# RoPE and scores: the last slot of three loads of k is brought in by two small transfers of its own

## The chip, the cores and the metric
The kernel runs on one core of a Trainium2 chip. The metric is the device time of one execution in microseconds (us): the median of 6 runs of the kernel before is 800.83 us (800.23 to 801.45). One further execution was recorded by the hardware profiler. It took 801.19 us, of which 799.4 us lie between its first and its last instruction; that stretch is called the span.

## The reference, cut to what matters
Inputs are q and k of shape [16, 512, 16, 64] (batch, position, head, dimension) in float32 and two tables cos and sin of [512, 32].

```python
def rot(x):                                   # rotary embedding
    x1, x2 = x[..., :32], x[..., 32:]
    return concatenate([x1 * cos - x2 * sin, x1 * sin + x2 * cos], axis=-1)
scores = einsum('bshd,bthd->bsht', rot(q), rot(k))      # [16, 512, 16, 512] float32
```

The output has 268 MB, q and k together have 67 MB: for every byte read, four are written.

## The kernel before, in words
**Tiling.** A batch's 512 positions are laid out as 128 partitions times C = 4 slots, so that position 4p + c stands in partition p and slot c. One load (`load`, L79) brings a whole batch of q or of k, 128 rows of 16 KB in DRAM, into a tile of 128 partitions by 4 slots by 1024 numbers. A slot is thus 4 KB of each row. The output is made in 64 stages, one for each batch and slot; a stage makes 128 x 16 x 512 scores (4 MB) in a tile `st` of the pool `stage`, which has three buffers.

**A stage** (the main loop runs i from 4 to 63) runs over 8 pairs of heads. For each pair TensorE makes two products into PSUM (L166, weights are qT, moving data kT of the batch) and ScalarE copies the pair's scores into `st` (L173). In between, VectorE rotates one slot of q two stages ahead and one slot of k five stages ahead (L106, L107, L111), TensorE transposes a slot of q one stage ahead and a slot of k four stages ahead (L127), and VectorE and ScalarE copy these out of PSUM (L142). At the end of a stage the whole 4 MB are stored by one transfer (L147).

**Order.** Everything is in the order of the program (`manual_schedule`); each engine takes its instructions in that order. All loads and all stores of the main loop are issued by SyncE on one queue (called SPq in the profile), in this order for each batch: three stores, a load of q, a store, a load of k. The load of q for batch b is issued after the third stage of batch b - 2, the load of k for batch b after the last stage of batch b - 3. The pool `in` holds two tiles each of q and of k. A transfer over 128 rows is shared out over 16 DMA engines, 8 rows for each; every DMA engine takes its shares one after another in the order of issue, and each of them adds one to the transfer's semaphore when its share is done. There are eight such semaphores, used in turn.

**Where the waits are.** A store waits for ScalarE's last copy of its stage. A stage's first copy into `st` waits until the store that used this buffer, three stages back, has landed in full, that is, on all 16 engines. A load waits for VectorE and TensorE to have done with the tile that it replaces.

**The last store** is cut in three (L151 to L153): the first 14 heads over all 128 rows, and the last two heads first for 116 rows and then for 12. The three lines that the change repeats in a load have this form already:

```python
nc.sync.dma_start(o[:, :h], st[:, :h])          # L151
nc.sync.dma_start(o[:116, h:], st[:116, h:])    # L152
nc.sync.dma_start(o[116:, h:], st[116:, h:])    # L153
```

Of the kernel before, what the change touches and what calls it, by code (L numbers as in the profile page):

```python
# [10 lines left out]
def kernel(  # L11
# [8 lines left out]
    nc = tc.nc  # L20
# [4 lines left out]
    B, S, H, D = q.shape  # L25
    HD = D // 2
    P = 128
    C = S // P
    HP = H // 2
    NST = B * C  # L30
    G = H // C

    const_pool = ctx.enter_context(tc.tile_pool(name="const", bufs=1))
# [9 lines left out]
    dram = {  # L43
        "q": q.rearrange("b (p c) h d -> b p c h d", c=C),
        "k": k.rearrange("b (p c) h d -> b p c h d", c=C),
    }
# [15 lines left out]
    def load_units(which, head, heads):  # L62
        n = C * heads * D
        t = early[:, used[0] : used[0] + n].rearrange("p (c e) -> p c e", c=C)
        used[0] += n
        src = dram[which][0, :, :, head : head + heads, :]
        nc.sync.dma_start(t.rearrange("p c (h d) -> p c h d", d=D), src)
        for h in range(0, heads, G):
            units[which, (head + h) // G] = t[:, :, D * h : D * (h + G)]

    batches = {}

    def load(which, b):

        if b >= B:
            return
        t = in_pool.tile([P, C, H * D], fp32, tag=which + "_in", name=which + "_sb")
        batches[which, b] = t
        nc.sync.dma_start(t.rearrange("p c (h d) -> p c h d", h=H), dram[which][b])  # L79

    def rope(which, n):


        part = part_pool.tile([P, H * D], fp32, tag="part", name="part")
        if n < C:
            x = units[which, n]
            sv, k1, k2 = "p c (g j) -> p c g j", {"j": HD}, {"j": D}
            cs = cos_t.unsqueeze(2).to_broadcast((P, C, 2 * G, HD))
            ss = ss_v.unsqueeze(2).to_broadcast((P, C, G, D))
            pv = part.rearrange("p (c g j) -> p c g j", c=C, j=D)  # L90
            x5 = x.rearrange("p c (h x j) -> p c h x j", x=2, j=HD)
            p5 = part.rearrange("p (c h x j) -> p c h x j", c=C, x=2, j=HD)
            adds = [(x5[:, :, :, y], p5[:, :, :, 1 - y]) for y in range(2)]
        else:
            x = batches[which, n // C][:, n % C]
            sv, k1, k2 = "p (g j) -> p g j", {"j": HD}, {"j": D}
            cs = cos_t[:, n % C].unsqueeze(1).to_broadcast((P, 2 * H, HD))
            ss = ss_v[:, n % C].unsqueeze(1).to_broadcast((P, H, D))
            pv = part.rearrange(sv, **k2)
            x4 = x.rearrange("p (h x j) -> p h x j", x=2, j=HD)  # L100
            swapped = bass.AP(part.tensor, part.offset + HD, [part.ap[0], (D, H), (-HD, 2), (1, HD)])
            adds = [(x4, swapped)]
        xs, xc = x.rearrange(sv, **k2), x.rearrange(sv, **k1)

        def products():
            nc.vector.tensor_tensor(pv, xs, ss, op=mult)  # L106
            nc.vector.tensor_tensor(xc, xc, cs, op=mult)  # L107

        def sums():
            for y, z in adds:  # L110
                nc.vector.tensor_tensor(y, y, z, op=add)  # L111

        return [products, sums]
# [30 lines left out]
    def store(i, st):  # L144
        o = o_v[i // C, i % C]
        if i < NST - 1:
            nc.sync.dma_start(o, st)  # L147
# [7 lines left out]
    def scores(i, p, st):  # L155
# [18 lines left out]
        if b == 0 and p % 2 == 1:  # L174
            c = p // 2
            nc.sync.dma_start(o_v[0, c, :, G * i : G * (i + 1)], st[:, G * c : G * (c + 1)])
        elif b > 0 and p == HP - 1:
# [10 lines left out]
    with tc.manual_schedule():  # L188
        for t, src in ((cos_t, cos), (sin_t, sin)):
            nc.scalar.dma_start(t, src.rearrange("(p c) j -> p c j", c=C))  # L190
        for head, heads in ((0, G), (G, H - G)):
            load_units("k", head, heads)
            load_units("q", head, heads)
        load("k", 1)
        load("q", 1)
        make_identity(nc, ident)
        nc.scalar.copy(out=ss_t[:, :, 0, :], in_=sin_t)
# [6 lines left out]
        for i in range(C):  # L204
            st = st_first[i] if i < 2 else stage_pool.tile([P, H, S], fp32, tag="stage", name="st")
            if i < C - 1:
                dve = rope("k", i + 1) + rope("q", i + 1) + rope("k", C + i)
                nxt = [("k", i + 1), ("q", i + 1)]
            else:
                dve = rope("q", C) + rope("k", C + i) + rope("q", C + 1) + rope("k", 2 * C)  # L210
                nxt = [("q", C), ("k", C + i)]
            for p in range(HP):
                scores(i, p, st)
                if p in (0, 1) and i > 0:
                    run(dve[:1])
                    dve = dve[1:]
                    transposed("k", C + i - 1, p, nc.vector.tensor_copy)
                if p == 3 and i < 2:
                    load("kq"[i], 2)
                if p in (2, 6):  # L220
                    m = len(dve) - (4 if p == 2 else 2) - (2 if i == C - 1 else 0)
                    run(dve[:m])
                    dve = dve[m:]
                    tr_act(*nxt.pop(0))
            run(dve)
        load("k", 3)


        for i in range(C, NST):
            tr = {}  # L230
            if i + 1 < NST:
                tr[1], tr[3] = ("q", i + 1, 0), ("q", i + 1, 1)
            if i + C < NST:
                tr[5], tr[6] = ("k", i + C, 0), ("k", i + C, 1)
            dve = []
            if i + 2 < NST:
                dve += rope("q", i + 2)
            if i + 1 + C < NST:
                dve += rope("k", i + 1 + C)
# [46 lines left out]
```

## Time and profile before

| what | value |
|---|---|
| median of 6 runs | 800.83 us (800.23 to 801.45) |
| the profiled execution | 801.19 us, span 799.4 us |
| TensorE | busy 691.8 us (87%) |
| VectorE | busy 544.6 us (68%) |
| ScalarE | busy 561.9 us (70%) |
| 16 DMA engines, mean rate over the span | 421 GB/s |
| HBM | 67.24 MB read, 268.44 MB written |
| stores of 4 MB | 59, median 24.0 us from issue to landing |
| loads of k, of 2 MB | 15, median 28.4 us from issue to landing |
| loads of q, of 2 MB | 15, median 27.8 us from issue to landing |

Busy time is that of all instructions of an engine; a DMA share of 1.00 means that all 16 engines had packets under way all the time. The time from issue to landing includes the time for which a transfer stands in line behind those issued before it. Beside the busy times the trace has two records that are used below: each DMA packet with its start, duration and size (without the number of its engine), and each of the 16 additions to a transfer's semaphore with its time.

### The profile page before, as it was taken

The numbers are of one execution on the slowest core, as the hardware profiler recorded it, in microseconds if no ns is written. First come the engines' busy times: TensorE is split into PE (matmuls) and PEld (weight loads), VectorE is DVE, ScalarE is ACT, GpSimd is POOL, SyncE is SP. The second block draws the span as 40 slices with busy tenths as digits, with TensorE's granted clock in tenths as the row PEclk, the third lists the DMA queues.
The fourth block names the chain that finished last, engine by engine and source line by source line (L and its number), as shares of the span: only waits on it lengthen the run. The fifth ranks groups of instructions, "written<-read, shape, count | busy, mean of one in ns | idle before, by whom it ended". The sixth has DMA issues, their size and how long they took to land.

```text
span 799.4 us, 7715 instructions
## 1 busy us (share of the span) xinstructions
PE 691.8 (87%) x3072; PEld 300.3 (38%) x3072; DVE 544.6 (68%) x516; ACT 561.9 (70%) x647; POOL 0.7 (0%) x6
## 2 busy tenths in 40 slices
PE   3989999888979989797897978979789797899970
PEld 2444443333434334343343433434334343343430
DVE  6999988666766768585685856848668486685300
ACT  2978886775858668585785857758567685677870
POOL 0000000000000000000000000000000000000000
PEclk9999999998998999898998989989899898998995
DMA  9999999999999999999999999999999999998996
GB/s 348 391 427 429 436 422 430 426 429 439 423 437 423 428 436 424 437 425 432 433 423 440 430 432 427 434 429 432 432 428 433 424 409 440 422 443 355 419 430 264
DMA packets 17844, 336.17 MB, mean 421 GB/s; under 512 B 1808, under 2 KB 3088, under 8 KB 4240
## 3 DMA queue, kind: packets, MB, share of 16 engines
q1 hardware_dynamic: 17520, 335.55, 98.5%
q8 instruction: 24, 0.39, 0.2%
q10 hardware_dynamic: 288, 0.13, 0.1%
q14 instruction: 12, 0.10, 0.0%
HBM read 67.24 MB, written 268.44 MB: 420 GB/s over the span
## 4 chain that ended last, share of the span: by engine, by line
DMA 49%; PE 37%; DVE 5%; ACT 4%; issue 1%; ACTq 0%
DMA out_dram<-st 49%; PE ps L166 28%; PE bank L127 9%; ACT st L173 4%; DVE part L106 2%; DVE early L111 1%; DMA sin_t<-in_sin_dram 1%; DVE k_sb L111 1%; DVE k_sb L107 1%; DVE early L107 1%; DVE kT_t L142 0%; DVE q_sb L107 0%; DVE q_sb L111 0%; ACTq L281 0%; DVE qT_t L142 0%
## 5 line engine op out<-in xcount | busy, mean ns | idle before, releaser
L173 ACT COPY st<-ps 128x1024 f32<-128x1024 f32 x512 | 495.3, 1018 | 202.5 <-DMA out_dram<-st 109.0
L166 PE MATMUL ps<-kT_t,qT_t 64*128 64x512 f32 x2048 | 549.0, 654 | 69.8 <-ACT st L173 69.8
L166 PEld LDWEIGHTS ps<-kT_t,qT_t 64*128 64x128 f32 x2048 | 185.8, 198 | 258.7 <-issue 139.0
L142 DVE COPY qT_t<-bank 128x512 f32<-128x512 f32 x118 | 81.6, 691 | 202.4 <-PE bank L127 202.4
L127 PEld LDWEIGHTS bank<-ident,q_sb 128*128 128x128 f32 x480 | 55.8, 152 | 103.8 <-issue 101.2
L127 PE MATMUL bank<-ident,q_sb 128*128 128x128 f32 x480 | 87.3, 309 | 0.9 <-PE ps L166 0.9
L127 PEld LDWEIGHTS bank<-ident,k_sb 128*128 128x128 f32 x480 | 50.5, 141 | 95.2 <-DVE k_sb L107 37.1
L127 PE MATMUL bank<-ident,k_sb 128*128 128x128 f32 x480 | 78.7, 287 | 1.6 <-DVE qT_t L142 1.2
L142 ACT COPY kT_t<-bank 128x512 f32<-128x512 f32 x122 | 72.5, 598 | 6.2 <-PE bank L127 6.2
L107 DVE TENSOR_TENSOR q_sb<-q_sb,cos_t 128x1024 f32<-128x1024 f32 x60 | 73.5, 1226 | 2.1
L107 DVE TENSOR_TENSOR k_sb<-k_sb,cos_t 128x1024 f32<-128x1024 f32 x60 | 73.5, 1225 | 2.0
L111 DVE TENSOR_TENSOR k_sb<-k_sb,part 128x1024 f32<-128x1024 f32 x60 | 73.5, 1225 | 2.1
L106 DVE TENSOR_TENSOR part<-q_sb,ss_t 128x1024 f32<-128x1024 f32 x60 | 73.5, 1225 | 2.0
L106 DVE TENSOR_TENSOR part<-k_sb,ss_t 128x1024 f32<-128x1024 f32 x60 | 73.0, 1216 | 0.1
L111 DVE TENSOR_TENSOR q_sb<-q_sb,part 128x1024 f32<-128x1024 f32 x60 | 72.9, 1216 | 0.0
L127 PE MATMUL bank<-ident,early 128*128 128x128 f32 x64 | 10.5, 316 | 13.5 <-DVE early L111 11.6
L127 PEld LDWEIGHTS bank<-ident,early 128*128 128x128 f32 x64 | 8.3, 161 | 18.7 <-issue 15.4
L106 DVE TENSOR_TENSOR part<-early,ss_t 128x1024 f32<-128x1024 f32 x8 | 9.8, 1222 | 6.9 <-ACT ss_t L198 6.8
L111 DVE TENSOR_TENSOR early<-early,part 128x512 f32<-128x512 f32 x16 | 10.3, 687 | 0.2
L107 DVE TENSOR_TENSOR early<-early,cos_t 128x1024 f32<-128x1024 f32 x8 | 9.8, 1225 | 0.3
L142 ACT COPY qT_t<-bank 128x512 f32<-128x512 f32 x10 | 5.7, 617 | 3.2 <-PE bank L127 3.2
L142 DVE COPY kT_t<-bank 128x512 f32<-128x512 f32 x6 | 4.1, 685 | 1.1 <-PE bank L127 1.1
(9 smaller groups left out, 2.8 us busy)
## 6 DMA issues: line engine op xcount, KB each, us to landing
out_dram<-st SPq DMA_DIRECT2D x59, 4096.0 KB, 24.0
k_sb<-in_k_dram SPq DMA_DIRECT2D x15, 2048.0 KB, 28.4
q_sb<-in_q_dram SPq DMA_DIRECT2D x15, 2048.0 KB, 27.8
out_dram<-st SPq DMA_DIRECT2D x16, 1024.0 KB, 13.7
out_dram<-st SPq DMA_DIRECT2D x1, 3584.0 KB, 20.4
early<-in_k_dram SPq DMA_DIRECT2D x1, 1536.0 KB, 9.8
early<-in_q_dram SPq DMA_DIRECT2D x1, 1536.0 KB, 13.0
early<-in_k_dram SPq DMA_DIRECT2D x1, 512.0 KB
```

The lines of the kernel that those rows point to most:

```text
L106: nc.vector.tensor_tensor(pv, xs, ss, op=mult)
L107: nc.vector.tensor_tensor(xc, xc, cs, op=mult)
L111: nc.vector.tensor_tensor(y, y, z, op=add)
L127: nc.tensor.transpose(bank[:, x, :], src, ident)
L142: copy(out=dst, in_=src)
L166: nc.tensor.matmul(out=po, lhsT=lhs[64 * r : 64 * r + 64, :], rhs=rh, start=True, stop=True)
L173: nc.scalar.copy(out=so, in_=si)
```

## The change
In the loads of k for batches 9, 12 and 15, slots 0 to 2 are loaded by one transfer over 128 rows of 12 KB. Slot 3 follows in two transfers: rows 0 to 115, and rows 116 to 127, each row 4 KB. The other 12 loads of k that go through `load`, and all loads of q, are as before. The bytes moved, the tile and all work of the other engines stay as they are; SyncE issues six transfers more, and the use of the eight semaphores shifts along with them.

```diff
+    UNEVEN = (9, 12, 15)
 ...
         t = in_pool.tile([P, C, H * D], fp32, tag=which + "_in", name=which + "_sb")
         batches[which, b] = t
-        nc.sync.dma_start(t.rearrange("p c (h d) -> p c h d", h=H), dram[which][b])
+        d = t.rearrange("p c (h d) -> p c h d", h=H)
+        src = dram[which][b]
+        if which == "k" and b in UNEVEN:
+
+            nc.sync.dma_start(d[:, : C - 1], src[:, : C - 1])
+            nc.sync.dma_start(d[:116, C - 1], src[:116, C - 1])
+            nc.sync.dma_start(d[116:, C - 1], src[116:, C - 1])
+        else:
+            nc.sync.dma_start(d, src)
```

## The prediction
> **What bounds the kernel now.** I read the DMA part of the page first, then the waits, then the busy time in chosen stretches, and last the trace's records of single packets and of the additions to each transfer's semaphore.
>
> The DMA part of the page and the list of waits:
>
> ```profile
> DMA  9999999999999999999999999999999999998996
> ...
> q1 hardware_dynamic: 17520, 335.55, 98.5%
> q8 instruction: 24, 0.39, 0.2%
> ```
>
> ```profile
> PEld ps L166 <- ACT st L173: 115.8, 113, 5.2
> ACT st L173 <- DMA out_dram<-st: 109.0, 35, 5.6
> ```
>
> The DMA engines are full in nearly every slice. ScalarE waits for stores to free a buffer of `st`, and TensorE waits for ScalarE. So transfers set the pace. Which of them, the stretches show (columns: start:end, length, then busy us and instruction counts of PE, PEld, DVE, ACT, POOL, then granted clock, DMA share and GB/s):
>
> ```profile
> 600.00:632.00 32.00, 29.14 (x126) 12.64 (x128) 23.76 (x22) 22.67 (x28) 0.00 (x0) 0.89 1.00 430
> ...
> 728.00:730.00 2.00, 2.00 (x12) 0.97 (x12) 1.93 (x3) 1.86 (x3) 0.00 (x0) 1.00 0.31 131
> 730.00:732.80 2.80, 2.80 (x15) 1.10 (x13) 1.07 (x1) 2.65 (x5) 0.00 (x0) 1.00 0.19 82
> 732.80:740.00 7.20, 7.20 (x38) 3.31 (x38) 4.87 (x5) 6.02 (x8) 0.00 (x0) 1.00 1.02 430
> ...
> 792.00:796.00 4.00, 0.00 (x0) 0.00 (x0) 0.00 (x0) 0.00 (x0) 0.00 (x0) 0.50 0.31 122
> 796.00:799.40 3.40, 0.00 (x0) 0.00 (x0) 0.00 (x0) 0.00 (x0) 0.00 (x0) 0.50 0.04 16
> ```
>
> To 632 us all 16 engines work without a gap. At 728 to 732.8 us most stand idle, and yet some go on; and at the end the last 4 us belong to very few. The engines have drifted apart. The semaphore additions say how far. The store issued at 616.9 us lands first at 633.6 us, and on the 16 engines with these lags behind the first: 0, 0, 0.1, 0.2, 0.5, 1.6, 2.5, 2.8, 2.9, 2.9, 2.9, 3.7, 5.1, 5.2, 6.3 and 12.0 us. One engine is alone at the back. Following packets end to start, its 32 KB store packets take 1.243 us on the mean of the stretch from 74 to 632 us where the others take 1.213; its loads are no slower. Its landings follow each other at 9.9 us a store without a gap, while the fastest, at 9.7, run dry when the next store is issued late:
>
> ```profile
> 695.86 72.44 SPq L147 DMA_DIRECT2D out_dram<-st  x8
> 777.83 0.33 SPq L151 DMA_DIRECT2D out_dram<-st  x1
> 778.75 0.68 SPq L152 DMA_DIRECT2D out_dram<-st  x1
> 779.48 1.17 SPq L153 DMA_DIRECT2D out_dram<-st  x1
> ```
>
> The chain is: the slow engine's share of a store lands, a buffer is free, a stage is made, the next store is issued. At the end the slow engine lands last, at 798.4 us; the engines that hold the 116 rows of L152 land theirs at 796.0 to 796.7 and their last row at 796.9; the rest are done by 792.7.
>
> **What the Trainium skill says.** "DMA: Bandwidth & Descriptors", "Why a DMA increments its semaphore by 16 and not by 1": a transfer from SyncE runs on the largest number of engines up to 16 that divides its row count, the lowest-numbered ones, so 116 rows run on 4 (29 rows each) and 12 rows on 12. The trace agrees: L152 has four additions that come with data, L153 twelve. Same page, "Latency and other measured facts": engines 7 and 15 are usually slower. The trace does show one slow engine. L153's twelve additions include one at 798.4 us and L152's four do not, so it is one of engines 4 to 11. "Runtime: NRT & Kernel Launch", "Instruction fetch mechanics": instructions come in 16 KB blocks by DMA; the trace has 24 such packets, and each holds up one DMA engine by about 1.3 us (0.94 us before the next packet and about 0.4 in it). These are part of the lags above.
>
> **The change part by part.**
>
> *Relief of engines 4 to 11.* A 16 KB load row is recorded at 0.611 us and follows the last by 0.607: 8 rows are 4.86 us. After: 8 rows of 12 KB, estimated at 0.75 x 0.607 = 0.455 us, are 3.64, one 4 KB row is 0.155 (recorded 0.159 in L152), together 3.80. The slow engine gains 1.06 us a load, 3.2 us in three. Engines 12 to 15 gain 1.2 a load.
>
> *Charge on engines 0 to 3.* 3.64 + 29 x 0.155 + 0.155 = 8.29 us for 4.86: 3.43 us more a load, 10.3 us in three. From below nothing speaks for less: L152's packets never took under 0.159. From above: L152's four shares took 5.3 to 6.0 us where 29 x 0.155 is 4.5, stalled at their start while other engines finished; if each of the three loads stalls alike, 3 x 1 us more. I take 10.3 and keep 13.3.
>
> *Issues.* Two more on SyncE per load, 0.7 to 1.2 us each as in L152 and L153. The next instruction there is a store that is issued some 9.6 us after the load (357.75 after 348.16), and waits for ScalarE; behind it nothing is delayed. If that cover were gone it would be 2 us a load. The eight semaphores in turn: each transfer waits for the one eight before it, which was issued about 50 us earlier and lands within some 30; nothing.
>
> *Use of the tile.* Slot 3 of the load issued at 348 us is rotated more than 50 us later and lands at about 382: nothing.
>
> *What is late next: the first four engines.* Their own work from 633.6 us on, for an engine with lag L there: 13 stores of 9.70 (8 x 1.213), 3 loads of 4.87, the 28 KB rows 8.5 (8 x 1.062): 149.2, so 782.8 + L. (Before, the first landing of these rows is at 790.6: the difference was idle, 1.4 us at 634, 5.4 at 728, the rest small.) With the charge 793.1 + L, with L152's and L153's rows 5.5 (the shortest now): 798.6 + L. This work is without gaps and can't be done sooner. Before, the end was 798.4. So the end moves by 0.2 + L, L being the largest lag among engines 0 to 3. The slow engine would be done at 798.4 - 3.2 = 795.2, which then sets nothing.
>
> *L.* The packet records carry no engine number. Four drawn from the 15 have a largest lag up to 1.6 in 15 of 1365 draws, up to 3.7 in 36%, up to 5.2 in 73%, 6.3 in 27%. The 16 KB fetches hit eight engines in turn, three rounds, and the slow one is not among them; if these are engines 0 to 7 in order, the first four have lags 5.2, 2.9, 6.3 and 3.7. I take L = 5.5: the sum is +5.7 us on a span of 799.4 and on 801.19 us of the profiled execution, which is 0.36 above the median of the runs. 800.83 + 5.7 gives 806.5.
>
> **The rivals.**
> 1. *The first four are the front group* (lags to 0.5, five engines): the fetches would have to spare them. Then the end moves by 0.2 to 0.7: 801 to 801.6. For it: on the last stores, where lags are 0.6 to 1.9 us, every late engine is one of 4 to 11. Against it: those lags come from two or three fetches only. A transfer that doesn't run on four engines would also end here.
> 2. *Faster: the relief reaches the end.* The slow engine then ends at 795.2, 797.7 us in all. It decides if the four end before 796.8: they would have to be ahead of what the trace shows for the very first engine by 1.8 us, or the 4 KB rows to be that much cheaper. For it: the idle time at 728 us, and the slow engine's place. Against it: three charges of 3.43 are more than the 7.8 us that any engine stands idle from 633 us on.
> 3. *Slower still:* the 116 rows stall in each load, and L = 6.3: 13.3 - 10.3 + 6.5 = 9.5, 810.3.
>
> **How the numbers follow.** Forecast, the four engines last with L from 1.5 to 6.3 and stalls to 1.5 us: 0.73, own range 802.5 to 809; rival 1: 0.14; rival 2: 0.07; rival 3: 0.06. A difference of 0.2% (1.6 us) is about what a measurement here can tell. Faster 0.07, same 0.14, slower 0.79. The range 801.0 to 809.3 leaves out rival 2, part of rival 1 and most of rival 3.
>
> **What would show it.** In the profile after: transfers of k of 1536, 464 and 48 KB, three each. The idle stretch at 728 us is filled to a quarter (4 of 16 engines) or more. In the last microseconds the four engines end together with a spread like their lags, several us after the slow one, and the last landing is the 116 or 12 rows', not L151's. It is wrong if the slow engine still lands last (then the charge or the lag is too large), or if L151's landings show the first four in front at 790 us. SyncE's waits and TensorE's busy time should not move.

## The result, and the profile after

The changed kernel takes 803.57 us (median of 15 runs, 802.21 to 806.34), beside 800.96 us for the kernel before in the same comparison (33 runs). The ratio is 1.0035, 95% interval 1.0027 to 1.0044: slower by 2.8 us by the ratio (2.6 between the medians), where 5.7 were forecast. The profiled execution took 803.57 us, with a span of 801.8 us.

The DMA part of the page, of the changed kernel:

```profile
DMA  9999999999999999999999999999999999999994
...
q1 hardware_dynamic: 17952, 335.55, 98.3%
q8 instruction: 24, 0.39, 0.2%
```

The same bytes move. The one 8 that stood at 728 us is gone, and the last slice has fallen from 6 to 4: what was idle in the middle is filled, and the end is emptier. The transfers issued, from the same view:

```profile
k_sb<-in_k_dram SPq DMA_DIRECT2D x12, 2048.0 KB, 23.1
...
k_sb<-in_k_dram SPq DMA_DIRECT2D x3, 1536.0 KB, 27.7
...
k_sb<-in_k_dram SPq DMA_DIRECT2D x3, 464.0 KB
...
k_sb<-in_k_dram SPq DMA_DIRECT2D x3, 48.0 KB
```

The waits, and the queue at the end:

```profile
PEld ps L175 <- ACT st L182: 123.0, 113, 7.4
ACT st L182 <- DMA out_dram<-st: 118.1, 37, 7.9
```

```profile
697.80 69.20 SPq L156 DMA_DIRECT2D out_dram<-st  x8
775.18 0.33 SPq L160 DMA_DIRECT2D out_dram<-st  x1
776.10 0.28 SPq L161 DMA_DIRECT2D out_dram<-st  x1
776.43 0.89 SPq L162 DMA_DIRECT2D out_dram<-st  x1
```

ScalarE waits 9 us more for stores in all. Yet the last store is issued 2.65 us sooner than before (775.18 for 777.83). Issue is early and landing late, so the loss lies in the DMA engines' own queues. The stretches (columns as in the prediction):

```profile
728.00:730.00 2.00, 2.00 (x12) 0.81 (x8) 1.43 (x2) 1.40 (x2) 0.00 (x0) 1.00 0.73 311
730.00:732.80 2.80, 2.80 (x15) 1.39 (x16) 2.00 (x3) 2.80 (x4) 0.00 (x0) 1.00 0.96 410
...
792.00:796.00 4.00, 0.00 (x0) 0.00 (x0) 0.00 (x0) 0.00 (x0) 0.00 (x0) 0.50 0.28 117
796.00:801.80 5.80, 0.00 (x0) 0.00 (x0) 0.00 (x0) 0.00 (x0) 0.00 (x0) 0.50 0.15 59
```

The additions to the semaphores say whose the end is. The shares of L160 (28 KB rows, all 16 engines) land from 787.6 us on; the last five come at 793.7, 794.3, 795.7, 796.0 and 796.3. Four of these five are engines 0 to 3: the four shares of L161 land at 798.2, 799.1, 800.2 and 800.8, each 4.5 to 4.9 us after one of them, and the last rows of L162 on these engines at 798.4 to 800.95. The fifth, at 796.0, is the slow engine, with its row of L162 at 796.2. Before, it landed these at 798.2 and 798.4. So the relief came (2.2 us), and the last of the four engines now ends 4.8 us behind it.

### The profile page after: what moved, and what is told of

It is laid out like the page before. It is cut to its first block, busy times and chain, and to the rows that moved or that the text cites. A ratio compares the mean times of both kernels' runs of the same rounds, so it can differ in the third digit from the quotient of the medians.

```text
span 801.8 us, 7727 instructions
## 1 busy us (share of the span) xinstructions
PE 684.6 (85%) x3072; PEld 296.5 (37%) x3072; DVE 544.5 (68%) x516; ACT 560.8 (70%) x647; POOL 0.7 (0%) x6
## 4 chain that ended last, share of the span: by engine, by line
DMA 49%; PE 35%; DVE 7%; ACT 5%; issue 1%; ACTq 0%
DMA out_dram<-st 48%; PE ps L175 27%; PE bank L136 8%; ACT st L182 5%; DVE part L115 2%; DVE early L116 1%; DVE early L120 1%; DVE k_sb L120 1%; DVE k_sb L116 1%; DMA sin_t<-in_sin_dram 0%; DVE kT_t L151 0%; DVE q_sb L116 0%; DVE q_sb L120 0%; ACTq L290 0%; DVE qT_t L151 0%
## 5 line engine op out<-in xcount | busy, mean ns | idle before, releaser
L175 PE MATMUL ps<-kT_t,qT_t 64*128 64x512 f32 x2048 | 542.9, 647 | 75.6 <-ACT st L182 75.6
L175 PEld LDWEIGHTS ps<-kT_t,qT_t 64*128 64x128 f32 x2048 | 182.6, 195 | 264.1 <-issue 136.6
```

The lines of the kernel that those rows point to most:

```text
L175: nc.tensor.matmul(out=po, lhsT=lhs[64 * r : 64 * r + 64, :], rhs=rh, start=True, stop=True)
```

## The experiments

The theory (A): every DMA engine has its own sum of work, and the last one sets the end; the change puts 3.47 us on engines 0 to 3 and takes 1.06 us from the slow engine, per load. The first rival (B): a load cut in three costs by itself, through issues, semaphores and small rows. A second rival (C) came out of the run with five uneven loads. In the diffs, lines with - are the changed kernel's; in the last-rows run they are those of the kernel before.

**The cut without the imbalance.**

```diff
-            nc.sync.dma_start(d[:116, C - 1], src[:116, C - 1])
-            nc.sync.dma_start(d[116:, C - 1], src[116:, C - 1])
+            nc.sync.dma_start(d[:112, C - 1], src[:112, C - 1])
+            nc.sync.dma_start(d[112:, C - 1], src[112:, C - 1])
```

> The three loads stay cut in three transfers, but slot 3 is cut at row 112 in place of 116, so that both parts run on all 16 DMA engines (7 rows and 1 row each); no engine gets more than before. Theory A (the time is lost because engines 0 to 3 get 3.45 us more work per load and end last): as before, 800.2 to 801.8 us. Rival B (a load in three transfers costs by itself: two more issues on SyncE, the shifted semaphores, 4 KB rows in place of 16 KB): as the changed kernel, 802.5 us or more.

Measured: 801.03 us, beside 801.03 for the kernel before; ratio 0.9997 (0.9987 to 1.0007). The transfers are there, and the DMA slices are those of the kernel before, with the 8 and the 6 at the end:

```profile
DMA  9999999999999999999999999999999999998996
...
k_sb<-in_k_dram SPq DMA_DIRECT2D x3, 1536.0 KB, 28.8
...
k_sb<-in_k_dram SPq DMA_DIRECT2D x3, 448.0 KB, 29.2
```

Rival B falls. Three transfers instead of one, the shifted semaphores and the 4 KB rows cost nothing that shows (the interval leaves room for 0.6 us); it is where the rows go.

**Two uneven loads, and one.**

```diff
-    UNEVEN = (9, 12, 15)
+    UNEVEN = (9, 12)        # second run: (9,)
```

> Only the loads for batches 9 and 12 are uneven, not 15. Theory A: the end is the later of two sums. Engines 0 to 3: 3.5 us sooner than in the changed kernel, last landing about 797.5 us. The slow engine: 1.06 us later than there, about 797.4. Both before the 798.4 of the kernel before, so about 1 us faster than before: 799.2 to 800.6. Rival B (each cut load costs about 0.9 us): 802.7.

> Only the load for batch 9 is uneven. Theory A: engines 0 to 3 have idle time for one charge of 3.5 us, the slow engine is relieved by 1.06 us and still lands last: 0 to 1 us faster than before, 799.8 to 801. Rival (each uneven load costs 0.9 us): 801.9.

Measured: with two, 800.66 us beside 801.03, ratio 1.0009 (0.9996 to 1.0023); no difference can be claimed, and the median is 0.1 us over the band named. Its 22 runs fall in two groups, 15 from 799.9 to 801.5 and 7 from 803.0 to 808.0. The profiled one (805.14 us) is of the second: three of the four engines land L161 at 796.1 to 797.8 us, as theory A has it, the fourth at 802.2. That one was 3.4 to 4.2 us behind the other three already when they began on the 116 rows for batch 9; why is not known. With one load, 800.26 us beside 800.73, ratio 0.9989 (0.9982 to 0.9996): faster by 0.9 us by the ratio (0.5 between the medians), about the relief of one load (1.06). Here the four end by 794.1 us and the slow engine, at 796.9, is last again.

**Five uneven loads.**

```diff
-    UNEVEN = (9, 12, 15)
+    UNEVEN = (3, 6, 9, 12, 15)
```

> Uneven loads for batches 3, 6, 9, 12 and 15. Theory A: two charges of 3.47 us more on engines 0 to 3 than in the changed kernel, and nothing else in the way: 803.6 + 6.9 = 810.5 us (809 to 812). Rival B: 0.9 us for each cut load, 805.3.

Measured: 817.89 us, ratio 1.0196 (1.0173 to 1.0218). The direction is A's, but the two loads more cost 14.3 us (between the medians) where two charges are 6.9: the band that A named, 809 to 812 us, was missed. The DMA slices show more than the end:

```profile
DMA  9999999999999999999899999998999999898994
GB/s 347 421 424 420 437 423 437 426 433 434 427 434 430 433 430 427 431 421 431 375 394 430 432 430 424 402 426 345 410 431 431 434 394 434 384 415 361 434 427 198
```

From the middle on the rate dips again and again (375, 345, 384, 361 GB/s). In the store at 405.24 us twelve engines begin in the same 0.14 us, having run dry. The last packet of such a store, just ahead of the load issued next, takes 1.8 to 2.4 us instead of 1.213, on 8 to 12 engines within 0.5 us (at 414.7, 514.0, 568.1 and 667.4 us), and about 10 us later on the four late engines too. Such packets of 32 KB over 1.8 us number 57 here, 17 in the changed kernel and 6 in the kernel before. Hence rival C: with the four engines far behind, the others run dry early (that is, they have nothing left to move until the next store is issued) and start again in step, and in step packets are slower, for the four as well.

**Three uneven loads, earlier and later.**

```diff
-    UNEVEN = (9, 12, 15)
+    UNEVEN = (3, 6, 9)      # second run: (13, 14, 15)
```

> Three uneven loads as in the changed kernel, but for batches 3, 6 and 9. Theory A in its plain form (only the sum of work on engines 0 to 3 counts, not its place): as the changed kernel, 802.6 to 804.6 us. Rival C, from the five-load run, which was 7 us over plain theory A: early uneven loads put engines 0 to 3 last sooner, the other twelve run dry and start again in step with each other, and packets in step take longer: 805 us or more.

> Three uneven loads, for batches 13, 14 and 15. Plain theory A (only the sums count): as the changed kernel, 802.6 to 804.6 us. Rival C (the time in which engines 0 to 3 are last, and the others run dry and restart in step, costs extra): the four fall behind only in the last 200 us, less extra than in the changed kernel: 800.5 to 802.5 us.

Measured: early 808.75 us, ratio 1.0089 (1.0068 to 1.0109); late 802.92 us, ratio 1.0031 (1.0020 to 1.0042). The same work at an earlier place costs 4 to 5 us more (4.3 by the ratios, 5.2 between the medians), so the sum alone is not the whole of it, and plain A fails for the early place. The late place can't be told from the changed kernel (the intervals of the ratios overlap): C's gain of 1 us or more did not come, and plain A holds there. Long packets number 47 in the early run and 8 in the late one. One such spot in the early run, in stretches and in SyncE's queue:

```profile
403.58 0.33 SPq L156 DMA_DIRECT2D out_dram<-st  x1
404.01 0.72 SPq L88 DMA_DIRECT2D k_sb<-in_k_dram  x1
413.60 0.33 SPq L156 DMA_DIRECT2D out_dram<-st  x1
```

```profile
403.50:404.80 1.30, 1.30 (x10) 0.50 (x6) 0.00 (x0) 1.30 (x3) 0.00 (x0) 1.00 1.14 492
404.80:413.00 8.20, 8.20 (x40) 3.74 (x42) 7.35 (x8) 6.87 (x9) 0.00 (x0) 1.00 0.99 408
413.00:414.50 1.50, 1.50 (x9) 0.54 (x6) 1.20 (x1) 1.50 (x3) 0.00 (x0) 1.00 0.91 295
414.50:420.00 5.50, 5.50 (x29) 2.54 (x29) 4.43 (x5) 4.41 (x5) 0.00 (x0) 1.00 0.96 369
```

After the late store at 403.58 us every engine is busy (share 0.91 to 0.99), and yet 408, 295 and 369 GB/s move where a steady stretch moves 430. Eleven packets of this store take over 1.8 us from 411.8 us on. Busy engines that move less: that is C's loss.

How much of it the four late engines bear can be worked out by following their packets end to start from 100 us to the last. In the early run they stand idle for at most 2.1 us in all that time. But against the steady 1.213 us for a 32 KB store packet and 0.611 us for a 16 KB load row, their packets take 8.4 to 9.4 us longer in sum, 5.2 to 5.9 of it in load rows. In the changed kernel the same sum is 2.9 to 3.7 us on the three of the four that can be followed. The difference is the time lost: the four did not run out of work, their packets were slower.

Why they were slower is argued, not shown. Being in step when a store gives way to a load fits. The kernel before has such a place too, with no engine made late: six engines, most of which had run dry for a moment, begin a store within 0.15 us at 633.8 us, and five last packets of this store, ahead of the load of q, take 1.9 to 2.3 us at 642.4 us. Being in step alone is not enough: of the store issued there at 731.96 us, whose first 14 shares land within 0.2 us and behind which no load follows, no packet takes more than 1.81 us. No run changed the step alone.

**The imbalance at other places: last store whole; cut at row 68.**

```diff
-        if i < NST - 1:
-            nc.sync.dma_start(o, st)
-            return
 ...
+        nc.sync.dma_start(o, st)      # for every stage
```

> The three uneven loads are kept, and the last store is one transfer over 128 rows on all 16 engines. Theory A: what counts is the sum on each engine, so engines 0 to 3 lose the 4.67 us of the small rows at the end and gain 1.2 us in the whole store (797.5 us for their last landing), the slow engine gains 1.0 (797.4): 799.2 to 800.8 us in all. Rival B (the loads themselves cost the time): 803 us or more.

```diff
-            nc.sync.dma_start(d[:116, C - 1], src[:116, C - 1])
-            nc.sync.dma_start(d[116:, C - 1], src[116:, C - 1])
+            nc.sync.dma_start(d[:68, C - 1], src[:68, C - 1])
+            nc.sync.dma_start(d[68:, C - 1], src[68:, C - 1])
```

> The three loads are cut at row 68 in place of 116: 68 rows run on 4 engines (17 rows each), 60 rows on 15 (4 rows each). Charge on engines 0 to 3 per load: 13 rows more than the 8 before, 2.0 us in place of 3.47; relief of engines 4 to 14: 4 rows, 0.62 us. Theory A (two sums, the later one sets the end): engines 0 to 3 land at 800.95 - 10.4 + 6.05 = 796.6 us, the slow engine at 796.3 + 3.2 - 1.9 = 797.6: faster than before by about 1 us, 799.2 to 800.6. Rival (uneven loads cost whatever their size): 802 or more.

Measured: with the last store whole 800.88 us, ratio 1.0002 (0.9993 to 1.0011). The three uneven loads are all there, and the loss is gone once the four engines are spared the small rows at the end: it is the sum on them that counted. (What a whole last store does to the kernel before was not run; A's sum has it from the charges above.) The time is 0.1 us over the band named. Cut at row 68: 800.86 us, ratio 0.9995 (0.9982 to 1.0008), again no difference, and again spread, 799.33 to 803.59; in the profiled execution (801.55 us) three of the four land L161 by 796.4 us and one at 798.8, the slow engine L160 at 797.7. The rival of a fixed price falls; the gain of 1 us is not reached in the median.

**Which is the slow engine.**

```diff
-        nc.sync.dma_start(o[116:, h:], st[116:, h:])
+        nc.sync.dma_start(o[116:124, h:], st[116:124, h:])
+        nc.sync.dma_start(o[124:, h:], st[124:, h:])
```

> The kernel before, with the last 12 rows of the last store cut in 8 rows (engines 0 to 7) and 4 rows (engines 0 to 3). If the slow engine is one of 4 to 7, the 8-row transfer lands last, some 0.2 us after the whole-row part, at about 798.4 us; if it is one of 8 to 11, the 8-row transfer lands with engines 0 to 3, by 797.2. Time as before, within 0.3 us.

Measured: 801.74 us, one run, 1.0 us above the kernel before in the same comparison, whose runs spread from 799.9 to 805.0; within 0.3 was expected. The 8-row transfer's last addition comes at 798.95 us, 0.18 after the whole-row part's last (798.77); its other seven come by 796.6. So the slow engine is one of 4 to 7 here. The experiments ran on three chips, and each of them has such an engine: in the profiles of the even split, of one load and of two late loads, 307 to 319 of the store packets between 74 and 632 us take between 1.225 and 1.3 us, where one engine moves about 365.

**Early by itself; two late.**

```diff
-    UNEVEN = (9, 12, 15)
+    UNEVEN = (3,)           # second run: (13, 15)
```

> One uneven load, for batch 3. The four engines stay ahead of the slow one all through, so nobody runs dry sooner than before: plain theory A and rival C both say as with batch 9 alone, 799.8 to 801, slightly faster than before. If an early place costs by itself (say through the first loads of k, which are needed sooner), 801.5 or more.

> Two uneven loads, for batches 13 and 15. Theory A: engines 0 to 3 end near 797.5 us, the slow one at 796.3 to 797.4, as with batches 9 and 12: 799.2 to 800.6 us. With rival C added, a little less than with 9 and 12 (800.66): 799.2 to 800.3.

Measured: one early, 799.57 us beside 800.86, ratio 0.9984 (0.9978 to 0.9991), 0.2 us below the band named. An early place alone costs nothing. That the early loads must be enough to make the four engines last fits this run and the one with three; two early loads were not run. Two late, 799.37 us, ratio 0.9982 (0.9973 to 0.9990): faster than both kernels, 1.5 us below the one before in the same comparison and 4.2 below the changed one, which was measured apart from it. In its profiled execution the four end L161 between 792.9 and 795.6 us and the slow engine is last at 796.2; the stretch that was idle is full, and the end is short:

```profile
728.00:733.00 5.00, 5.00 (x26) 2.21 (x24) 3.60 (x5) 3.94 (x6) 0.00 (x0) 1.00 0.98 419
787.00:792.00 5.00, 0.00 (x0) 0.00 (x0) 0.00 (x0) 0.00 (x0) 0.00 (x0) 0.50 0.30 125
792.00:797.20 5.20, 0.00 (x0) 0.00 (x0) 0.00 (x0) 0.00 (x0) 0.00 (x0) 0.50 0.15 60
```

## Why the prediction was right, and where its size was off

**Bound and direction: right.** One slow engine set the pace, the four engines that take the 116 rows became last, and the end is theirs. The place named for it, the last rows and not the whole-row part, is where it is seen, and the idle stretch at 728 us filled as said (shares 0.31 and 0.19 became 0.73 and 0.96).

**Charge: right.** In the load for batch 9 the four engines take 3.65 us for the 12 KB rows, and their 30 small rows 4.67 us on the two that don't stall: 8.32, where 8.29 was worked out. Stalls on the other two were 0.2 and 0.5 us. In the load for batch 15 the 12 KB rows take 4.2 to 4.6 us on the three engines that can be followed, so stalls of up to 1 us came, as the forecast allowed.

**Relief: right per load, short in sum.** One load gave 0.9 us by the ratio. In three, the slow engine's last landing moved by 2.2 instead of 3.2 us in the profiled executions.

**The edits costed at nothing: right.** The even cut measures them all at once: 0.9997.

**The lag L: the term that was mis-sized.** The forecast was 798.6 + L, with L = 5.5. The four engines end at 798.4, 799.3, 800.4 and 800.95, so L came to 2.4 for the last of them. It can be read more directly as well: of the store issued at 616.1 us, after two charges of 3.47, three of the four land 7.4, 9.0 and 9.6 us behind the first engine (the fourth can't be told apart), which leaves 0.5, 2.1 and 2.7 us as their own lag.

The step that failed is the reading of the fetches as falling on engines 0 to 7 in order, which put lags of 5.2 and 6.3 on the first four. The first row of the load for batch 9 shows the four 0.10, 0.12, 0.78 and 1.07 us behind the foremost engine, while two engines among 12 to 15 were 5 us back. And of the 14 fetches from 343 us on, 11 leave no trace on the three engines that can be followed; at the other three these are held up by at most 0.7 us, less than the shortest fetch takes (0.88). So L = 5.5 rested on a guess that did not hold; the range of 1.5 to 6.3 that was given with it took in what came.

Rival 1 was right that the four were near the front and wrong on the time, since they did not stay together: 1.0 us apart at batch 9, 2.6 at the end. The size of L is not fixed either. In the profiled run with two uneven loads one of the four was nearly 4 us behind its fellows at batch 9; that fits the wider spread of the runs, 4.1 us here.

**Last rows: a little too dear.** 5.5 us was taken from the kernel before for L152 and L153, where the engines' start was stalled by others that were finishing. In the changed kernel the others have long ended, and they take 4.7 to 5.0. This and the stalls in the load for batch 15 are of about the same size and of opposite sign, which is luck.

**What was not foreseen** is rival C, though the kernel before showed it: of the 1.4 us at 634 us that the prediction's sum books as idle time, the foremost engines stood idle for only about 0.5 (633.3 to 633.8 us); the rest went into their long last packets of that store. No part of it can be told apart here (the late three are no faster beyond the intervals), but it costs 4 to 5 us when the loads are early. One sign did not hold to the letter: TensorE's busy time, which was not to move, is 684.6 us where it was 691.8; the runs do not say why. Which engine the slow one is among 4 to 7, on which engines the fetches do fall, and why the lag of one of the four varies between executions stay open. The sentence on engines 7 and 15 that the prediction takes from the Trainium skill ("DMA: Bandwidth & Descriptors", "Latency and other measured facts") does not settle the first: the page calls that slowness, in a best guess, specific to transfers issued by GpSimd, and here SyncE issues the loads and stores.

## What to carry to other kernels

Where transfers bound a kernel, count the work of each DMA engine and not the mean of sixteen: the row count of a transfer decides how many engines share it, and the additions to its semaphore show who is ahead and who is last. Work can be moved off a slow engine in this way, but in these loads the 7 rows taken from it put 22 on each of the four engines that receive them, so stop while those still have idle time (two such loads late in the kernel gained 1.5 us, two at batches 9 and 12 nothing that can be claimed, three lost 2.8). Splitting a load as such was free here.

## What the runs showed of the hardware that was not expected

- One DMA engine, one of 4 to 7 in the run that narrows it down, takes 1.243 us for a 32 KB store packet where the others take 1.213; its loads are as fast as theirs. At the store issued at 616.9 us it lies 12 us behind the first.
- Engines that ran dry and start together on a store have its last packet, ahead of the next load, at 1.8 to 2.4 us instead of 1.213, 8 to 12 of them within 0.5 us (five uneven loads). Around one such spot (three early loads) the DMA share stays at 0.9 or more while the rate falls to 295 to 408 GB/s.
- An engine can lose time without ever being idle: three early uneven loads made the packets of the four late engines 8.4 to 9.4 us longer in sum, most of it in 16 KB load rows, where it was 2.9 to 3.7 us with the three loads at batches 9, 12 and 15.
